# Second layer's probability transfers issued by SyncE, and the last heads' outputs moved into the output projection

## Chip, core and metric

The kernel runs on one core of a Trainium2 chip. The metric is the time of one execution on the device, in microseconds (us); the kernel before takes 2298.8 us (median of three runs, 2298.3 to 2300.2). A difference of about 0.2% (4.6 us) is what a measurement of this kernel can tell from no change.

## What is computed

A two-layer decoder trunk on 272 tokens (16 meta tokens and 256 inputs), width 2048, 16 heads of 128. Layer 0 uses forgetting attention. Layer 1, where the change lies, uses stick-breaking attention with keys and values from `w_kv`, followed by an output projection and a squared-ReLU MLP:

```python
def stick_breaking_attention(q, k, v):
    scale = HEAD_DIM ** -0.5
    outs = []
    for qs, qe in query_blocks(q.shape[1]):
        z = jnp.einsum('bqhd,bkhd->bhqk', q[:, qs:qe], k[:, :qe]).astype(jnp.float32) * scale
        ...
        log_beta = jax.nn.log_sigmoid(z)
        log_one_minus = jnp.where(mask, jax.nn.log_sigmoid(-z), 0.0)
        suffix = lax.cumsum(log_one_minus, axis=3, reverse=True) - log_one_minus
        a = jnp.where(mask, jnp.exp(log_beta + suffix), 0.0).astype(v.dtype)
        outs.append(jnp.einsum('bhqk,bkhd->bqhd', a, v[:, :qe]))
    return jnp.concatenate(outs, axis=1)
...
o = stick_breaking_attention(q, shared_k, shared_v)
h = h + o.reshape(b, length, D_MODEL) @ sb_w_o[i]
h = h + squared_relu_mlp(rms_norm(h, norm_mlp[layer]), w_up[layer], w_down[layer])
```

## The kernel before

**Matrix products.** Activations lie feature-major in SBUF, 16 chunks of 128 features by 272 (or 256) tokens. Every operand is split into a high and a low part, and a product is the sum of three: high by high, high by low, low by high. `gemm_group` (L215) makes 512 output features in four accumulators: it walks the 2048 input features in four quarters (kb 0 to 3) of 48 products each, 192 in all. The text calls a quarter by its number. `weights` (L186) loads each quarter as two halves of 512 KB by SyncE (L199, tiles `raw`, four buffers, so two quarters ahead), and splits each half: ScalarE makes the high part (L210, `whi`) and VectorE the low part (L211, `wlo`), again with four buffers. A load waits until VectorE has split the half that was in its buffer; a split waits for its load and until TensorE has used the part that was in its buffer. In quarters 0 and 3 TensorE takes the accumulators one after the other; in 1 and 2 it takes the first half of the weights for all four and then the second.

**Second layer's attention.** The loop at L696 takes four heads at a time (g = 0 to 3: heads 0-3, 4-7, 8-11, 12-15). A group is: product with the key weights (`w_kv[2g]`), scores `pz` (L717, L718), softplus, scan and exponential on ScalarE and VectorE (L723 to L728) for two pairs of heads, and the product with the value weights (`w_kv[2g+1]`, L743). TensorE needs the probabilities with keys on the partitions. They are turned without TensorE: VectorE transposes blocks of 32x32 (L451, tile `raw_p`), four transfers write them to a scratch in HBM (`turn_probabilities`, L454, `p_dram`), and two transfers read them back in the other order (`probabilities_back`, L461), one of them into the same tile `raw_p`. All six for each pair are issued by ScalarE, whose queue is in order: an issue that has to wait keeps back what stands behind it. The values go the same way for the first three groups (`squares`; L401 writes `v_dram`, L406 reads it back), also issued by ScalarE. For the last four heads there is no such return; TensorE transposes V itself (`token_major`, L379).

**Outputs.** `outputs1` (L749) splits the returned probabilities (L370 on ScalarE, L371 on VectorE), reads the values back, multiplies (`po`, L420 and L769, and a corner product through `pvc`, L756 and L767) and writes the result into `ao` (L443, L444). For g = 0 to 2 it is called inside the next group's key product, ahead of quarter 3. For g = 3 it is called after the loop, ahead of the output projection (L774), whose first group (`out_proj`, L608) needs these heads only in quarter 3.

**Order of the work.** The program is built with a scheduler that orders each engine's instructions by its own estimates. `behind` (L171) adds an ordering edge without a semaphore, so that an instruction is placed behind a given product; `issued` holds the products of the current group. The transfers back are placed behind products 140 and 184 of the value product (L744), and the splits of the returned probabilities behind products 36 and 72 of the next group, or, for the last heads, behind the last product so far (L752). Each transfer signals on one of a small number of landing semaphores, used in turn; an instruction that would signal on one again waits until the earlier transfer on it has landed, whichever engine issued it.

Of the kernel before, what the change touches and what calls it, by code (L numbers as in the profile page):

```python
# [18 lines left out]
M = 16  # L19
# [10 lines left out]
G_A0, G_M0, G_KV, G_A1, G_M1, G_FIN = range(6)  # L30
# [3 lines left out]
def yoco_kernel(ctx: ExitStack, tc: tile.TileContext, hT_in, gains, b_f, w_f, w_qkv0, w_o0, w_up, w_dn,  # L34
                w_kv, w_q1, w_o1, g_row, out):
    nc = tc.nc
# [126 lines left out]
    queued, pinned, issued = [], [False], []  # L163
# [279 lines left out]
        nc.scalar.activation(hi, src, AF.Copy)  # L443
        nc.vector.tensor_tensor(out=lo, in0=src, in1=hi.bitcast(F32), op=ALU.subtract)  # L444

    def turn_probabilities(s, raw, pr):

        y = raw[:, :768].rearrange("p (c h b i) -> p c h b i", c=4, h=2, b=3)
        for i in range(2):
            for b, o in enumerate((0, 144, 144 + P)):  # L450
                nc.vector.transpose(y[:, :, i, b, :], s[:, 2 * pr + i, o:o + P].rearrange("p (c k) -> p c k", c=4))  # L451
        y = y.rearrange("p c h b i -> p c (h b i)")
        for a in range(4):
            nc.scalar.dma_start(p_dram[pr].rearrange("c j a x -> a j c x")[a], y[32 * a:32 * a + 32])  # L454

    def probabilities_back(pps, places):
        for pr, at in enumerate(places):
            raw, p0, p1 = pps[pr]
            back = p_dram[pr].rearrange("c j a (h x) -> (c j) (a h) x", h=2)
            for dst, src in ((raw[:, :512], back[:, :, :64]), (p1.rearrange("p i q -> p (i q)"), back[:, :, 64:])):  # L460
                behind(nc.scalar.dma_start(dst.rearrange("p (m x) -> p m x", m=8), src), issued[at])  # L461

    def in_order(p0, p1):

# [4 lines left out]
    ao = Split("o0", 0)  # L469
    for g in range(4):  # L470
# [71 lines left out]
        pps = []  # L542
        for pr in range(2):
            raw = att.tile([P, 2, 2, 256], F32, tag="pp", bufs=3, name=f"raw_p0_{g}_{pr}").rearrange("p x i q -> p (x i q)")
            p0 = att.tile([P, 2, 2, 256], F32R, tag="pp", bufs=3, name=f"p0_{g}_{pr}")
            p1 = tmp.tile([P, T], F32, tag="relu", name=f"p1_{g}_{pr}")[:, :2 * P].rearrange("p (i q) -> p i q", i=2)

            turn_probabilities(s, raw, pr)
            pps.append((raw, p0, p1))


# [10 lines left out]
        gemm_group(w_qkv0[3 * g + 2], xa, 0, lambda m, acc: evac_kv(m, acc, vT))  # L562


        probabilities_back(pps, (140, 176 if g else 191))

# [12 lines left out]
        for pr in range(2):  # L581
            raw, p0, p1 = pps[pr]
# [22 lines left out]
            outputs()  # L605


    def out_proj(w, ao, t0, gi, label):  # L608
        norm = Norm(label, t0)
        xm = Split(label, t0)  # L610
        for g in range(4):
            def evac(m, acc, g=g):
                c = 4 * g + m
                residual_add(c, acc, t0)
                split_chunk(xm, gi, c)
                norm.add(c)
            gemm_group(w[g], ao, t0, evac)
        return xm, norm

    def mlp(layer, xm, norm, t0, last_evac, last_group=None):  # L620
# [75 lines left out]
    for g in range(4):  # L696
        kT = att.tile([P, 4, T], F32, tag="kT", bufs=1, name=f"kT1_{g}")
        gemm_group(w_kv[2 * g], xc, 0, lambda m, acc: evac_kv(m, acc, kT), {3: outputs1} if g else {})
        q = qT1[g]

        k0 = att.tile([P, 4, T], F32R, tag="vT", bufs=1, name=f"k0_{g}")
        k1 = ao.spare[:, 4 * g:4 * g + 4]
        for j in range(0, 4, 2):
            nc.scalar.activation(k0[:, j:j + 2], kT[:, j:j + 2], AF.Copy)
            nc.vector.tensor_tensor(out=k1[:, j:j + 2], in0=kT[:, j:j + 2], in1=k0[:, j:j + 2].bitcast(F32),
                                    op=ALU.subtract)
        q2 = att.tile([P, 2, 4, P], F32R, tag="pp", bufs=3, name=f"q12_{g}")
        split(q2, q[:, :, P:S])
        z = att.tile([P, 4, 416], F32, tag="s", bufs=1, name=f"z_{g}")

        pps = []
        for pr in range(2):
            zp = z[:, 2 * pr:2 * pr + 2]
            for i in range(2):
                j = 2 * pr + i
                ps = patt.tile([P, 512], F32, tag="patt", name=f"pz_{g}_{j}")
                product = by_parts(ps[:, 144:416], [q2[:, k, j, :] for k in range(2)], [k0[:, j], k1[:, j]], True, True)  # L717
                placed_behind(nc.tensor.matmul(ps[:, 0:144], q[:, j, 0:P], kT[:, j, :144], start=True, stop=True), product)  # L718
                nc.vector.tensor_tensor(out=z[:, j], in0=ps[:, :416], in1=maskB, op=ALU.add)
            e, raw = (att.tile([P, 2, 2, 256], F32, tag="pp", bufs=3, name=f"{x}_{g}_{pr}")  # L720
                      .rearrange("p x i q -> p (x i q)") for x in ("e", "raw_p1"))
            e, sums = e[:, :832], raw[:, :832]
            softplus(e.rearrange("p (i k) -> p i k", i=2), zp)  # L723
            nc.vector.tensor_tensor_scan(out=sums, data0=goes_on.rearrange("p i k -> p (i k)"), data1=backward(e), initial=0.0,  # L724
                                         op0=ALU.mult, op1=ALU.add)
            zf = zp.rearrange("p i k -> p (i k)")
            nc.vector.tensor_tensor(out=zf, in0=zf, in1=backward(sums), op=ALU.subtract)  # L727
            nc.scalar.activation(zp, zp, AF.Exp)  # L728

            p0 = att.tile([P, 4, T], F32R, tag=("kT", "qT")[pr], bufs=(1, 4)[pr], name=f"p01_{g}_{pr}")  # L730
            p0 = p0.rearrange("p h t -> p (h t)")[:, :1024].rearrange("p (x i q) -> p x i q", x=2, i=2)
            p1 = tmp.tile([P, T], F32, tag="relu", name=f"p11_{g}_{pr}")[:, :2 * P].rearrange("p (i q) -> p i q", i=2)
            turn_probabilities(z, raw, pr)
            pps.append((raw, p0, p1))

        pm = patt.tile([P, 512], F32, tag="patt", name=f"pm1_{g}")
        placed_behind(nc.tensor.transpose(pm[:, 0:P], corners(z[:, :, P:144], z[:, :, 400:416], f"sm1_{g}"), ident), product)
        pm_sb = att.tile([P, 192], F32, tag="pm_sb", bufs=1, name=f"pm_sb1_{g}")
        nc.vector.tensor_tensor(out=pm_sb[:, :P].rearrange("p (b q) -> p b q", q=M), in1=maskD, op=ALU.mult,
                                in0=pm[:, P - M:P].unsqueeze(1).to_broadcast([P, 8, M]))  # L740

        vT = att.tile([P, 4, T], F32, tag="vT", bufs=1, name=f"vT1_{g}")
        gemm_group(w_kv[2 * g + 1], xc, 0, lambda m, acc: evac_kv(m, acc, vT))  # L743
        probabilities_back(pps, (140, 184))  # L744
        turned = squares(vT, "pp", f"1_{g}") if g < 3 else None
        if g < 3:
            scratch(turned, issued[-2:])

        def outputs1(g=g, vT=vT, pps=pps, pm_sb=pm_sb, turned=turned):  # L749
            for pr in range(2):  # L750
                raw, p0, p1 = pps[pr]
                behind(split(p0.rearrange("p x i q -> p x (i q)"), raw[:, :512]), issued[(36, 72)[pr] if g < 3 else -1])  # L752
            if turned is not None:
                vs = values_back(turned, issued[64:80:8], issued[112:128:8], f"1_{g}")
            pv = patt.tile([P, 512], F32, tag="patt", name=f"pvc_{g}")
            nc.tensor.transpose(pv[:, :P], corners(vT[:, :, P:144], vT[:, :, 256:T], f"vc1_{g}"), ident)  # L756
            vc_sb = att.tile([P, P], F32, tag="vm_sb", bufs=1, name=f"vc_sb_{g}")
            nc.scalar.copy(vc_sb, pv[:, :P])
            own = att.tile([P, 8, M], F32, tag="own", bufs=1, name=f"own1_{g}")
            for pr in range(2):  # L760
                v0, v1 = vs[pr] if turned is not None else token_major(vT, pr, 0, f"1_{g}_{pr}")
                po = patt.tile([P, 2, 256], F32, tag="patt", name=f"po1_{g}_{pr}")
                p0, p1 = in_order(*pps[pr][1:])
                for i in range(2):
                    product = weighted(po, v0, p0, i)
                    if pr == i == 0:
                        placed_behind(nc.tensor.matmul(pv[:, P:2 * P], vc_sb, pm_sb[:, :P], start=True, stop=True), product)  # L767
                        nc.scalar.copy(own, pv[:, P:2 * P].rearrange("p (c q) -> p c q", c=8))
                    nc.tensor.matmul(po[:, i, P:], v1[:, i, :], p1[:, i], start=False, stop=i == 1)  # L769
                ends = po.rearrange("p i (c q) -> p (i c) q", c=2)[:, :, P - M:]  # L770
                nc.vector.tensor_tensor(out=ends, in0=ends, in1=own[:, 4 * pr:4 * pr + 4], op=ALU.add)
                put_split(ao, 4 * g + 2 * pr, 2, M, S, po)

        if g == 3:  # L774
            outputs1()

    xm, norm_m = out_proj(w_o1, ao, M, G_M1, "m1")


    g_tok = att.tile([P, 4, T], F32, tag="kT", bufs=1, name="g_tok").rearrange("p h t -> p (h t)")[:, :512]  # L780
# [136 lines left out]
```

## Time and profile before

| | us |
|---|---|
| runs | 2298.3, 2298.8, 2300.2 |
| profiled execution | 2298.19 |
| its span (first to last instruction) | 2296.5 |
| TensorE busy in the span | 2269.9 |
| VectorE busy | 1344.9 |
| ScalarE busy | 1058.7 |
| mean granted TensorE clock | 0.995 of full |

PE is TensorE, DVE VectorE, ACT ScalarE, POOL GpSimd, SP SyncE; L210 is line 210 of the kernel. A "q" behind an engine's name (ACTq, SPq) is its sequencer, which issues transfers. In the view of waits a row reads: engine, tile and line that waited, what released it, then total us, number of times and the longest. In the view of windows a row reads: stretch, its length, busy us and instructions of PE, weight loads, DVE, ACT and POOL, then granted clock (1.00 is full), DMA share and GB/s. In a timeline a row reads: start, duration, engine, line, operation, written<-read tiles, count, and in brackets the engine's idle time before it with what ended it. The view of one tile gives, for each instruction on it, durations in ns (minimum/median/maximum).

### The profile page before, as it was taken

Reading aid. Unit: us, or ns where it says so; the run is one execution under the profiler, and the core shown is the slowest. Engines: PE = TensorE matmul, PEld = TensorE weight load, DVE = VectorE, ACT = ScalarE, POOL = GpSimd, SP = SyncE. Lnnn points to the kernel's source line nnn. Section 1 sums busy time; section 2 is a strip of 40 time slices with the busy share of each in tenths; the row PEclk is TensorE's granted clock in tenths of the full one; section 3 lists DMA queues with packets and bytes.
Section 4 is the critical chain, followed back from the end, with each engine's and each line's share of the span. In section 5 each row is a group of like instructions: output and inputs, shape, how many; then the busy total and the mean of one; then the engine's idle time right before and its main releaser. Section 6 shows DMA issues by size and latency. Waiting matters only on the chain.

```text
span 2296.5 us, 44901 instructions
## 1 busy us (share of the span) xinstructions
PE 2269.9 (99%) x18830; PEld 2260.0 (98%) x18830; DVE 1344.9 (59%) x1943; ACT 1058.7 (46%) x1451; POOL 36.7 (2%) x78
## 2 busy tenths in 40 slices
PE   9999999999999999999999999999999999999998
PEld 9999999999999999999999999999999999999998
DVE  7766666554554455455566677666555555555555
ACT  6444455443343344344454344455543543544554
POOL 0000000000000000000000000000000000000001
PEclk9999999999999999999999999999999999999999
DMA  7766765555555555555556566666666566566564
GB/s 238 226 197 192 221 184 170 183 174 182 173 183 180 171 185 175 182 175 179 181 177 199 174 187 182 176 197 201 188 190 202 186 200 199 187 200 191 186 202 139
DMA packets 167418, 431.46 MB, mean 188 GB/s; under 512 B 48800, under 2 KB 65072, under 8 KB 167216
## 3 DMA queue, kind: packets, MB, share of 16 engines
q1 hardware_dynamic: 113760, 406.29, 55.4%
q10 hardware_dynamic: 53456, 22.31, 4.0%
q8 instruction: 147, 2.41, 0.4%
q14 instruction: 55, 0.45, 0.1%
HBM read 416.99 MB, written 11.55 MB: 187 GB/s over the span
## 4 chain that ended last, share of the span: by engine, by line
PE 94%; DVE 2%; DMA 2%; issue 1%; ACTq 1%; ACT 0%; POOL 0%; POOLq 0%; SPq 0%; DVEq 0%
PE acc L177 91%; DMA raw_p<-p_dram 1%; DVE wlo L211 1%; DMA raw<-w_qkv 1%; PE po L420 0%; DVE raw_p L724 0%; DMA p_dram<-raw_p 0%; ACT whi L210 0%; ACTq L454 0%; DVE raw_p L451 0%; ACTq L401 0%; PE pz L420 0%; PE ps L420 0%; DVE z L727 0%; DVE e L693 0%
## 5 line engine op out<-in xcount | busy, mean ns | idle before, releaser
L211 DVE TENSOR_TENSOR wlo<-raw,whi 128x1024 fp32r<-128x1024 f32 (+1 forms) x773 | 927.4, 1216 | 730.4 <-ACT whi L210 722.4
L210 ACT ACTIVATE whi<-raw 128x1024 fp32r<-128x1024 f32 (+1 forms) x773 | 795.9, 1050 | 997.8 <-PE acc L177 904.2
L177 PE MATMUL acc<-x_m,whi 128*128 128x272 f32 (+1 forms) x4096 | 643.0, 281 | 0.0
L177 PE MATMUL acc<-x_u,whi 128*128 128x272 f32 (+1 forms) x3968 | 625.9, 281 | 0.0
L177 PEld LDWEIGHTS acc<-x_m,whi 128*128 128x128 f32 x4096 | 565.7, 188 | 0.1
L177 PEld LDWEIGHTS acc<-x_u,whi 128*128 128x128 f32 x3968 | 550.1, 188 | 0.0
L177 PE MATMUL acc<-x_m,wlo 128*128 128x272 f32 (+1 forms) x2048 | 440.7, 281 | 0.0
L177 PE MATMUL acc<-x_u,wlo 128*128 128x272 f32 (+1 forms) x1984 | 431.5, 281 | 0.0
L177 PE MATMUL acc<-x_a,whi 128*128 128x272 f32 (+1 forms) x2048 | 355.2, 286 | 0.7 <-ACT whi L210 0.5
L177 PEld LDWEIGHTS acc<-x_m,wlo 128*128 128x128 f32 x2048 | 323.2, 188 | 0.0
L177 PEld LDWEIGHTS acc<-x_u,wlo 128*128 128x128 f32 x1984 | 315.1, 188 | 0.0
L177 PEld LDWEIGHTS acc<-x_a,whi 128*128 128x128 f32 x2048 | 300.7, 188 | 2.6 <-ACT whi L210 1.7
L177 PE MATMUL acc<-x_a,wlo 128*128 128x272 f32 (+1 forms) x1024 | 253.4, 285 | 0.0
L177 PE MATMUL acc<-x_kv,whi 128*128 128x272 f32 x1024 | 199.5, 294 | 14.3 <-ACT whi L210 14.3
L177 PEld LDWEIGHTS acc<-x_kv,whi 128*128 128x128 f32 x1024 | 166.0, 195 | 15.1 <-ACT whi L210 15.1
L177 PEld LDWEIGHTS acc<-x_a,wlo 128*128 128x128 f32 x1024 | 175.5, 188 | 0.7 <-DVE ssq_a L143 0.4
L177 PE MATMUL acc<-x_o,whi 128*128 128x272 f32 (+1 forms) x1024 | 162.4, 282 | 0.0
L177 PE MATMUL acc<-x_kv,wlo 128*128 128x272 f32 x512 | 150.7, 294 | 1.6 <-DVE wlo L211 1.6
L177 PEld LDWEIGHTS acc<-x_o,whi 128*128 128x128 f32 x1024 | 142.0, 188 | 0.0
L292 DVE TENSOR_TENSOR hT<-acc,hT 128x272 f32<-128x272 f32 (+1 forms) x156 | 67.4, 432 | 75.4 <-PE acc L177 75.2
L177 PE MATMUL acc<-x_o,wlo 128*128 128x272 f32 (+1 forms) x512 | 110.8, 282 | 0.0
L177 PEld LDWEIGHTS acc<-x_kv,wlo 128*128 128x128 f32 x512 | 99.7, 195 | 2.5 <-DVE wlo L211 2.5
(220 smaller groups left out, 1042.4 us busy)
## 6 DMA issues: line engine op xcount, KB each, us to landing
raw<-w_up SPq DMA_DIRECT2D x256, 512.0 KB, 3.9
raw<-w_dn SPq DMA_DIRECT2D x256, 512.0 KB, 3.9
raw<-w_qkv SPq DMA_DIRECT2D x92, 512.0 KB, 4.1
raw<-w_o SPq DMA_DIRECT2D x64, 512.0 KB, 4.1
raw<-w_kv SPq DMA_DIRECT2D x64, 512.0 KB, 4.3
raw<-w_q SPq DMA_DIRECT2D x32, 512.0 KB, 4.7
p_dram<-raw_p ACTq DMA_DIRECT2D x64, 96.0 KB, 4.1
raw_p<-p_dram ACTq DMA_DIRECT2D x16, 256.0 KB, 6.7
```

What stands on the lines that cost most here:

```text
L177: ins = nc.tensor.matmul(*args, **kw).ins
L210: on_act = nc.scalar.activation(hp, src, AF.Copy)
L211: on_dve = nc.vector.tensor_tensor(out=lp, in0=src, in1=hp.bitcast(F32), op=ALU.subtract)
L292: nc.vector.tensor_tensor(out=hT[:, c, t0:], in0=acc, in1=hT[:, c, t0:], op=ALU.add)
```

## The change

Two edits. `turn_probabilities` and `probabilities_back` take the issuing queue as an argument: layer 0 passes ScalarE's as before, layer 1 passes SyncE's. And `outputs1` of the last heads is no longer called ahead of the output projection but inside its first group, ahead of quarter 1, with its two splits placed behind products 20 and 40 of that group. The values' transfers (L401, L406) stay on ScalarE.

```diff
-    def turn_probabilities(s, raw, pr):
+    def turn_probabilities(s, raw, pr, queue):
...
-            nc.scalar.dma_start(p_dram[pr].rearrange("c j a x -> a j c x")[a], y[32 * a:32 * a + 32])
+            queue.dma_start(p_dram[pr].rearrange("c j a x -> a j c x")[a], y[32 * a:32 * a + 32])
...
-    def probabilities_back(pps, places):
+    def probabilities_back(pps, places, queue):
...
-                behind(nc.scalar.dma_start(dst.rearrange("p (m x) -> p m x", m=8), src), issued[at])
+                behind(queue.dma_start(dst.rearrange("p (m x) -> p m x", m=8), src), issued[at])
...
-    def out_proj(w, ao, t0, gi, label):
+    def out_proj(w, ao, t0, gi, label, before={}):
...
-            gemm_group(w[g], ao, t0, evac)
+            gemm_group(w[g], ao, t0, evac, before if g == 0 else {})
...
-            turn_probabilities(z, raw, pr)
+            turn_probabilities(z, raw, pr, nc.sync)
...
-        probabilities_back(pps, (140, 184))
+        probabilities_back(pps, (140, 184), nc.sync)
...
-                behind(split(p0.rearrange("p x i q -> p x (i q)"), raw[:, :512]), issued[(36, 72)[pr] if g < 3 else -1])
+                behind(split(p0.rearrange("p x i q -> p x (i q)"), raw[:, :512]), issued[((36, 72) if g < 3 else (20, 40))[pr]])
...
-        if g == 3:
-            outputs1()
-
-    xm, norm_m = out_proj(w_o1, ao, M, G_M1, "m1")
+    xm, norm_m = out_proj(w_o1, ao, M, G_M1, "m1", {1: outputs1})
```

More of the change, by code (lines that the diff above doesn't have):

```diff
@@ L546, in yoco_kernel @@
             p1 = tmp.tile([P, T], F32, tag="relu", name=f"p1_{g}_{pr}")[:, :2 * P].rearrange("p (i q) -> p i q", i=2)
-            turn_probabilities(s, raw, pr)
+            turn_probabilities(s, raw, pr, nc.scalar)
             pps.append((raw, p0, p1))
@@ L562, in yoco_kernel @@
         gemm_group(w_qkv0[3 * g + 2], xa, 0, lambda m, acc: evac_kv(m, acc, vT))
-        probabilities_back(pps, (140, 176 if g else 191))
+        probabilities_back(pps, (140, 176 if g else 191), nc.scalar)
         pv = patt.tile([P, 512], F32, tag="patt", name=f"pvm_{g}")
```

## Prediction

> **What bounds the kernel now.** I read the page's first lines, then TensorE's waits in the second layer (span 1236 to 1512 us), then the stretches around them, then ScalarE's timeline inside the longest.
>
> ```profile
> span 2296.5 us, 44901 instructions
> PE 94%; DVE 2%; DMA 2%; issue 1%; ACTq 1%; ACT 0%; POOL 0%; POOLq 0%; SPq 0%; DVEq 0%
> ...
> PE acc L177 <- ACT whi L210: 14.3, 3, 5.8
> PE pvc L756 <- POOL pk_vc L438: 2.7, 1, 2.7
> PE acc L177 <- DVE wlo L211: 1.6, 3, 0.7
> ...
> 1293.05:1354.50 61.45, 55.20 (x431) 54.64 (x430) 40.89 (x67) 28.40 (x37) 1.71 (x4) 0.94 0.64 181
> 1354.50:1415.20 60.70, 55.71 (x430) 55.15 (x430) 40.81 (x67) 28.40 (x37) 1.77 (x4) 0.94 0.65 182
> 1415.20:1476.00 60.80, 56.06 (x431) 55.60 (x430) 40.89 (x67) 28.50 (x37) 1.87 (x4) 0.94 0.63 182
> 1323.70:1328.50 4.80, 4.36 (x18) 4.04 (x19) 4.80 (x5) 3.93 (x6) 0.00 (x0) 0.50 0.81 243
> 1383.90:1389.90 6.00, 5.56 (x23) 5.24 (x24) 5.72 (x6) 3.90 (x6) 0.00 (x0) 0.50 0.88 262
> 1445.30:1451.40 6.10, 6.10 (x27) 6.10 (x28) 4.51 (x5) 3.66 (x7) 0.00 (x0) 0.50 0.93 285
> 1498.40:1501.00 2.60, 0.00 (x0) 0.00 (x0) 1.24 (x3) 1.17 (x2) 0.41 (x2) 1.00 0.59 121
> ```
>
> TensorE is the bound; only its waits and its clock can be won. In the second layer it waits 14.3 + 1.6 us in three places, one for each of heads 0-3, 4-7 and 8-11, and 2.7 us once at the last heads. In the rows of windows the last three columns are granted clock, DMA share and GB/s. Behind each of the three waits the clock is 0.50, for 4.36, 5.56 and 6.10 us of busy time: half of that, 8.0 us, is lost too. The 2.7 us wait left the clock at 1.00. Check: each group's stretch less its own wait and half-clock loss (61.45 - 6.25 - 2.18, 60.70 - 4.99 - 2.78, 60.80 - 4.74 - 3.05; the single waits are in the next fence) is 53.0, 52.9 and 53.0 us, the same work three times. So **24.0 us** lie in three groups and **2.7 us** at the last one.
>
> ```profile
> 1302.56 2.21 ACTq L454 DMA_DIRECT2D p_dram<-raw_p  x4
> ...
> 1308.92 0.54 ACTq L461 DMA_DIRECT2D raw_p<-p_dram  x1
> 1309.50 0.68 ACTq L461 DMA_DIRECT2D p<-p_dram  x1
> 1310.33 6.32 ACTq L454 DMA_DIRECT2D p_dram<-raw_p  x4
> 1316.75 2.39 ACTq L401 DMA_DIRECT2D v_dram<-turned  x5
> 1319.26 0.53 ACTq L461 DMA_DIRECT2D raw_p<-p_dram  x1
> ...
> 1322.53 1.06 ACT L210 ACTIVATE whi<-raw 128x1024 fp32r<-128x1024 f32 x1 [14.86 <-DMA raw_p<-p_dram]
> ...
> 1323.64 0.82 PE L177 MATMUL acc<-x_kv,whi 128*128 128x272 f32 x2 [5.81 <-ACT whi L210]
> ...
> 1383.81 0.60 PE L177 MATMUL acc<-x_kv,whi 128*128 128x272 f32 x1 [4.55 <-ACT whi L210]
> ...
> 1444.00 0.52 PE L177 MATMUL acc<-x_kv,whi 128*128 128x272 f32 x2 [3.99 <-ACT whi L210]
> 1445.26 0.60 PE L177 MATMUL acc<-x_kv,wlo 128*128 128x272 f32 x1 [0.75 <-DVE wlo L211]
> ```
>
> The cause stands in ScalarE's queue (the short second waits are 0.75 in the third group, and the rest of 1.6, so 0.44 each, in the other two). An issue that has to wait for an earlier transfer (L461 for L454's landing, the second L454 for its transposes) keeps every later ScalarE instruction waiting. The weight split L210 of the next group's second quarter (kb 1) stands behind all of them and comes 14.86 us late.
>
> **The change part by part.** Removed from ScalarE in each of four groups: 8 issues L454 and 4 issues L461. The same 12 go to SyncE, between weight loads. The instruction order built from the changed program shows the rest. On ScalarE the split of kb 1's first half now stands ahead of all value issues L401, so it can run when TensorE has left the buffer that it reuses, one quarter (48 products) earlier. TensorE wants it at 1317.57 + 0.27 = 1317.84.
>
> ```profile
> 1301.26 1.27 DVE L451 STREAM_TRANSPOSE raw_p<-z 128x128 f32<-128x128 f32 x6
> ...
> 1309.03 1.27 DVE L451 STREAM_TRANSPOSE raw_p<-z 128x128 f32<-128x128 f32 x6
> ...
> 1317.57 0.27 PE L756 MATMUL pvc<-ident,pk_vc 128*128 128x128 f32 x1
> ...
> 1308.80 0.33 SPq L199 DMA_DIRECT2D raw<-w_kv  x1
> ...
> L454 ACTq DMA_DIRECT2D p_dram<-raw_p x32: 315/478/4042, 1302.6 to 1499.9; - x32
> ...
> L211 DVE TENSOR_TENSOR wlo<-raw,whi x48: 1180/1219/1227, 1294.2 to 1469.9; 128x1024 fp32r<-128x1024 f32 x48
> DMA to landing us min/median/max: 3.4/4.3/6.7
> ...
> L401 ACTq DMA_DIRECT2D v_dram<-turned x24: 309/454/916, 1316.7 to 1442.3; - x24
> DMA to landing us min/median/max: 1.7/2.2/3.1
> ...
> 428.32 756.84 PE acc L177 x6144
> 1599.71 533.27 PE acc L177 x4704
> ```
>
> (The two landing rows are those of the weight tiles and of the value tiles; a product takes 756.84 / 6144 = 0.123 us with 272 columns, 533.27 / 4704 = 0.113 us with 256.) Three new couplings have to be priced, on the first group's clock. A time from the median issue comes first; after the slash, one in which SyncE is held 4.04 us behind L461, as ScalarE was once (maximum of the L454 row).
>
> 1. **Weights behind transfers on SyncE.** L461 of pair 0 waits for L454's landing; I keep the 1308.9 of before, since transposes and transfer are the same. It takes 1.2 us to issue. Behind it stand the loads of kb 2, until now issued by 1308.80: now about 1310.5 / 1314.3, landed 4.3 us later at 1314.8 / 1318.6. Kb 2 is wanted at 1317.84 + 48 x 0.123 = 1323.8, so this alone costs nothing.
> 2. **Values behind those weights on ScalarE.** Landing semaphores are shared in turn, so in the new order the last L401 of pair 0 waits for the second kb 2 load, and the split of kb 1's second half stands behind it. It would end at 1314.8 + 0.45 + 1.06 = 1316.3 / 1320.1, and VectorE's half 1.22 us later at 1317.5 / 1321.4. TensorE wants them at 1317.84 + 24 x 0.123 = 1320.8 and 1321.0. Cost 0 / 0.4 us. Kb 2's split then follows a 0.6 us split of probabilities and four more L401, which wait for the first ones' landing (2.2 us): about 1320 / 1323 for ScalarE's part, 1324.1 at the latest for VectorE's, against 1323.8: 0 / 0.3 us.
> 3. **Last pair at the products `po`.** L461 of pair 1 waits for its L454 (transposes end 1310.3; issued by 1312.8 / 1316.5; 4.1 us more to L461, as from 1302.56 + 2.21 to 1308.92), so it issues near 1316.9 / 1320.6, against 1319.26 before. Kb 3's first load comes behind its 1.2 us (and the 4.04 us) and lands near 1322.8 / 1330.2; the value return L406 of pair 1 stands behind that load's split and takes 2.2 us and 0.8 us of its own split, so these values are there by about 1325.8 / 1333.2. `po` of pair 1 runs near 1317.84 + 96 x 0.123 + 1 = 1330.7. Cost 0 / 1.8 us beyond the 0.7 of step 2.
>
> So each group keeps 0 to 2.5 us. I take 0.5, near the lower end, because only one of 32 issues took 4 us. No single wait then reaches 2.67 us, after which the clock was still 1.00 (1498.40 row), so the 8.0 us of half clock go as well. Sum for three groups: 24.0 - 3 x 0.5 = **22.5 us**. VectorE and ScalarE can follow: 40.89 and 28.40 us of work in 53.
>
> [...]
>
> **The last heads.** Here the second L454 follows a split that waits 8.09 us for L461's landing, and VectorE stands behind the same split with the last quarter of V, so POOL's corner copy and `pvc` are late.
>
> ```profile
> 1485.50 2.03 ACTq L454 DMA_DIRECT2D p_dram<-raw_p  x4
> ...
> 1498.55 0.63 ACT L370 ACTIVATE p<-raw_p 128x512 fp32r<-128x512 f32 x1 [8.09 <-DMA raw_p<-p_dram]
> ...
> 1501.96 0.54 ACTq L461 DMA_DIRECT2D raw_p<-p_dram  x1
> ...
> 1505.86 0.64 ACT L370 ACTIVATE p<-raw_p 128x512 fp32r<-128x512 f32 x1
> ...
> 1500.59 0.42 POOL L438 COPY pk_vc<-vT 128x64 f32<-128x64 f32 x2 [5.50 <-DVE vT L480]
> ...
> 1501.06 0.33 PE L756 MATMUL pvc<-ident,pk_vc 128*128 128x128 f32 x1 [2.67 <-POOL pk_vc L438]
> ```
>
> Called after kb 0, with the splits placed behind products 20 and 40, V's last quarter goes ahead of the split and `pvc` stands after 48 products instead of 32: the 2.67 us go. In their place the first `po` stands after product 85 and needs a value split that is queued on ScalarE behind pair 1's probabilities. The group's first product ran at 1498.38 - 32 x 0.113 = 1494.8 and product 85 ends near 1494.8 + 9.6 + 0.5 (my estimate for `pvc` and four transposes) = 1504.9. By step 3, moved on by 1485.50 - 1302.56 = 182.9, L461 of pair 1 issues near 1499.8 / 1503.5, against 1501.96 before; it has landed at most 3.9 us later (1501.96 to 1505.86), and two splits take 1.0: the values are there at 1504.7 / 1508.4. New wait 0 to 3.5 us; I take 1.2, nearer the lower end for the reason given. Net gain 2.7 - 1.2 = **1.5 us**. Quarter 3 wants the last heads only after product 144, some 2 us after they are done.
>
> **Sum.** 22.5 + 1.5 = 24.0 us. The profiled execution took 2298.2 us (span 2296.5 and 1.7 around it), 0.6 under the median of the three runs. 2298.2 - 24.0 = **2274.2 us**.
>
> **The rivals.**
> *Waits come back elsewhere.* Steps 2 and 3 at their upper ends, 2.5 us in each of three groups, and as much lost at the last heads as won: 24.0 - 7.5 = 16.5, giving 2281.7; with the clock drop in one group (3 us) 2285. For it: steps 2 and 3 leave about 1 to 3 us of room at the medians. Against: TensorE no longer meets ScalarE's 14.86 us.
> *It only saves the issuing.* The transfers get no faster, and if ScalarE still stands as long for L401's landings, only 8 x 0.478 + 2 x 1.22 = 6.3 us of issue leave its queue; the waits of 4 to 5.8 us just go, unless the loads slip by as much. If they do slip, waits and half clock stay and only the last heads' 1.5 us are won: 2296.7.
> [...]
> *Slower: SyncE's order starves kb 1.* The mechanism of step 2, further on: if the second kb 2 load lands after about 1319.3, TensorE waits from 1320.8. It loses what was won (8.0 us a group) when the landing is near 1324.3 (5 us of wait and 3 of half clock). At 1327, 8 us and 3 in each group: 3 x 3 us slower, 2307. Against: that is 8 us behind the upper bound above, and more than any landing row shows.
>
> **How the numbers follow.** Forecast case (2271.5 to 2278): 0.64. Waits elsewhere (2278 to 2287): 0.22. Only the issuing (2294 to 2298): 0.06. Slower: 0.08. The range must leave out no more than 0.2: 2271.5, where nothing is left of all 26.7 us, less 0.5 for the run, is 2271; above it reaches into the second case, to 2285. A measurement here tells 0.2%, 4.6 us, from no change: faster 0.87, same 0.05, slower 0.08.
>
> **What would show it.** ScalarE's 14.86 us before L210 gone; windows of the three groups near 53 to 55 us with clock 1.00; TensorE's waits for L210 under 1 us each; a wait of 1 to 2 us before `po` (L420) in the output projection's first group; L454 and L461 as SyncE issues. Wrong if the clock shows 0.50 again there, or if SyncE's loads of kb 2 land after 1319 on the first group's clock.

## The result and the profile after

| | before | changed |
|---|---|---|
| median of 4 runs each, same chip, us | 2299.5 (2298.3 to 2301.7) | 2274.1 (2273.6 to 2274.6) |
| ratio, 95% interval | | 0.9888 (0.9871 to 0.9906) |
| profiled execution, us | 2298.2 | 2274.0 |
| mean granted clock | 0.995 | 1.000 |

The changed kernel is 1.1% faster, by 24.2 us between the two profiled executions; the prediction said 24.0 and 2274.2 us. The number holds. Its parts hold less well, as the runs below show.

First the changed kernel's span, then all waits of TensorE in the second layer (engine, tile, line, releaser; total us, times, longest), then the windows of the three groups (length; busy us of PE, weight loads, DVE, ACT, POOL; clock, DMA share, GB/s):

```profile
span 2272.3 us, 44903 instructions
```

```profile
PE po L420 <- ACT v L370: 0.9, 1, 0.9
PE po L420 <- DVE v L371: 0.2, 1, 0.2
```

```profile
1293.42:1346.90 53.48, 53.16 (x430) 52.76 (x429) 40.69 (x67) 28.93 (x38) 1.76 (x4) 1.00 0.70 207
1346.90:1400.40 53.50, 53.26 (x431) 52.85 (x430) 40.73 (x67) 29.02 (x38) 1.76 (x4) 1.00 0.67 207
1400.40:1453.10 52.70, 52.70 (x430) 52.70 (x430) 40.64 (x67) 28.90 (x38) 1.76 (x4) 1.00 0.70 210
```

The reader is to see three things. Not one wait for L210 or L211 is left. The groups take 53.5, 53.5 and 52.7 us where they took 61.5, 60.7 and 60.8, close to the 53 us that the prediction had worked out as the work alone. And the clock is 1.00 in all three. (The view of waits lists only larger ones; the groups' remainders at `po` are 0.32, 0.24 and 0 us, the first two read as length less busy time.) The first group starts at 1293.42 instead of 1292.5, so 0.9 us were lost ahead of it, in work that the change doesn't touch. That is spread: in `e1` below, which differs from neither ahead of this place, the group starts at 1291.8.

ScalarE's timeline (start, us, engine, line, operation, written<-read, count, idle time before it and what ended it) shows the new order in the first group:

```profile
1311.79 1.06 ACT L210 ACTIVATE whi<-raw 128x1024 fp32r<-128x1024 f32 x1 [2.48 <-PE acc L177]
1312.54 4.18 ACTq L401 DMA_DIRECT2D v_dram<-turned  x4
1316.84 1.06 ACT L210 ACTIVATE whi<-raw 128x1024 fp32r<-128x1024 f32 x1 [4.00 <-DMA p_dram<-raw_p]
...
1319.52 2.01 ACT L210 ACTIVATE whi<-raw 128x1024 fp32r<-128x1024 f32 x2 [1.10 <-DMA v_dram<-turned]
1322.01 0.34 ACTq L406 DMA_DIRECT2D turned<-v_dram  x1
```

The first half of the kb 1 split runs at 1311.79 as soon as TensorE frees its buffer; before, it ran at 1322.53, after 14.86 us. The second half stands behind four value issues that take 4.18 us in all: the wait that the prediction called coupling 2, real, and ended in time. On SyncE, in order:

```profile
1307.31 0.61 SPq L461 DMA_DIRECT2D raw_p<-p_dram  x1
...
1308.71 1.93 SPq L199 DMA_DIRECT2D raw<-w_kv  x2
1311.07 2.13 SPq L454 DMA_DIRECT2D p_dram<-raw_p  x4
1318.13 0.53 SPq L461 DMA_DIRECT2D raw_p<-p_dram  x1
```

The two L199 are the loads of kb 2. The profile gives one landing for them, 6.2 us after the issue, and the second issue began at 1310.2. So that load was there at about 1316.4, between the prediction's 1314.8 and 1318.6; the fourth value issue, which waits for it in the built program, left at 1316.4.

### The profile page after: what moved, and what is told of

Same layout as the page of the kernel before. It is cut to its first block, busy times and chain, and to the rows that moved or that the text cites. A ratio compares the mean times of both kernels' runs of the same rounds, so it can differ in the third digit from the quotient of the medians.

```text
span 2272.3 us, 44903 instructions
## 1 busy us (share of the span) xinstructions
PE 2263.1 (100%) x18830; PEld 2254.2 (99%) x18830; DVE 1344.1 (59%) x1943; ACT 1060.1 (47%) x1451; POOL 37.5 (2%) x78
## 4 chain that ended last, share of the span: by engine, by line
PE 95%; DMA 2%; DVE 1%; issue 0%; ACT 0%; SPq 0%; ACTq 0%; POOL 0%; POOLq 0%; DVEq 0%
PE acc L177 93%; DMA p_dram<-raw_p 1%; DMA turned<-v_dram 1%; DMA raw<-w_qkv 1%; PE po L420 0%; DMA raw_p<-p_dram 0%; ACT whi L210 0%; DVE wlo L211 0%; PE ps L420 0%; PE pz L420 0%; DMA raw<-w_kv 0%; DMA v_dram<-turned 0%; DVE raw_p L451 0%; PE pz L718 0%; PE ps L516 0%
## 5 line engine op out<-in xcount | busy, mean ns | idle before, releaser
L211 DVE TENSOR_TENSOR wlo<-raw,whi 128x1024 fp32r<-128x1024 f32 (+1 forms) x773 | 927.6, 1216 | 704.9 <-ACT whi L210 697.7
L210 ACT ACTIVATE whi<-raw 128x1024 fp32r<-128x1024 f32 (+1 forms) x773 | 796.4, 1050 | 966.1 <-PE acc L177 912.8
L177 PE MATMUL acc<-x_kv,whi 128*128 128x272 f32 x1024 | 193.9, 288 | 0.0
L177 PEld LDWEIGHTS acc<-x_kv,whi 128*128 128x128 f32 x1024 | 160.7, 188 | 0.0
```

Source lines behind the costliest of these rows:

```text
L177: ins = nc.tensor.matmul(*args, **kw).ins
L210: on_act = nc.scalar.activation(hp, src, AF.Copy)
L211: on_dve = nc.vector.tensor_tensor(out=lp, in0=src, in1=hp.bitcast(F32), op=ALU.subtract)
```

## The experiments

The theories, as they stood when the runs were chosen:

- **A**: ScalarE's issues that wait for landings (L461 above all) made the kb 1 split late; taking them away gives three groups' waits and half clock, about 23 us, and the last heads' move some 2 us.
- **B**: the move of the last heads paid.
- **C**: only the issuing time that leaves ScalarE counts, the rival "It only saves the issuing" that the prediction weighed.
- **A2**, formed after the first four runs: what counts is which issues the kb 1 split stands behind on ScalarE, whichever engine issues the probabilities.
- **D**, its rival: the probabilities must leave ScalarE.

### The two edits apart

`e1`: the queues alone. From the kernel before, with both helpers taking the queue as in the change:

```diff
-            turn_probabilities(z, raw, pr)
+            turn_probabilities(z, raw, pr, nc.sync)
...
-        probabilities_back(pps, (140, 184))
+        probabilities_back(pps, (140, 184), nc.sync)
```

> Only the issuing queue changes: the second layer's probability transfers (L454, L461) go to SyncE, the last heads stay ahead of the output projection. Theory A (waits inside ScalarE's issues made the kb 1 split late): the three groups' waits at TensorE (15.9 us) fall under 1 us in all, the clock stays at 1.00, so 2299.5 - 23.4 = about 2276 us, with the 2.7 us wait at pvc mostly still there. Theory B (the last heads' move is what paid): about 2297 us. Theory C (only issuing time counts): all issues of the second layer have left ScalarE here, so 2276 too; this run does not tell A from C.

Measured: 2273.6 us, ratio 0.9886 (0.9871 to 0.9901). This is the whole gain, with nothing left for the move. TensorE's waits in its second layer, then two instructions around the last heads (ScalarE, GpSimd):

```profile
PE po L420 <- ACT v L370: 2.4, 3, 1.1
```

```profile
1471.43 0.63 ACT L370 ACTIVATE p<-raw_p 128x512 fp32r<-128x512 f32 x1 [1.75 <-DMA raw_p<-p_dram]
```

```profile
1473.82 2.27 POOL L438 COPY pk_vc<-vT 128x64 f32<-128x64 f32 x2 [0.42 <-DVE vT L480]
```

There is no wait at `pvc` any more, although the last heads are where they were. The split that stood 8.09 us for the returned probabilities stands 1.75, V's last quarter is not held behind it, and the corner copy comes in time: the same delay of the transfers had fed that wait too. The 2.4 us that are left stand at `po` of the first two groups, where the expectation had under 1 us in all. B falls.

`e2`: the move alone (the edits of L749 and L774 of the diff, every transfer on ScalarE).

> Only the last heads' outputs move into the first group of the output projection; all transfers stay on ScalarE. Theory A: the three waits for L210 of 4 to 5.8 us and the stretches of clock 0.50 stay, the 2.7 us at pvc go and a wait of 0 to 3.5 us before po comes: 2296 to 2300 us, most likely near 2297.7 (1.8 us won, as in the changed kernel). Theory B: about 2276 us.

Measured: 2295.4 us, ratio 0.9988 (0.9978 to 0.9997).

```profile
PE acc L177 <- ACT whi L210: 13.8, 3, 5.0
PE acc L177 <- DVE wlo L211: 1.9, 3, 0.7
PE po L769 <- ACT v L383: 1.0, 1, 1.0
```

The three groups are as before; 2.7 us at `pvc` have become 1.0 at `po`. The move is worth something only as long as the transfers are late: 3.1 us between the medians alone, none on top of the queues.

### Half of the queues

Both with the move, and one of the two helpers on SyncE.

```diff
-            turn_probabilities(z, raw, pr, nc.sync)
+            turn_probabilities(z, raw, pr, nc.scalar)
```

> The move of the last heads, and of the queues only the transfers back (L461) on SyncE; the writes L454 stay on ScalarE. In the instruction order ScalarE still issues both L454 and all value issues L401 ahead of the kb 1 split, but no longer stands for L454's landing. Theory A: the split comes near 1319 us on the first group's clock instead of 1322.5, TensorE waits 1.5 to 3 us in each group and the clock stays at 1.00: 2278 to 2283 us. Theory C (the gain goes with the issuing time that leaves ScalarE, of which L461 is 2 x 1.22 of 6.3 us a group): 1.8 + 0.39 x 22.3 = 10.5 us won, 2289 us.

Measured: 2295.4 us, ratio 0.9983 (0.9973 to 0.9992): both theories missed. TensorE's waits, ScalarE's and SyncE's timelines:

```profile
PE acc L177 <- ACT whi L210: 11.8, 3, 4.5
PE acc L177 <- DVE wlo L211: 1.9, 3, 0.7
PE po L420 <- ACT v L370: 1.8, 1, 1.8
```

```profile
1309.71 1.92 ACTq L454 DMA_DIRECT2D p_dram<-raw_p  x4
1312.13 8.41 ACTq L401 DMA_DIRECT2D v_dram<-turned  x8
1320.64 1.06 ACT L210 ACTIVATE whi<-raw 128x1024 fp32r<-128x1024 f32 x1 [13.73 <-DMA v_dram<-turned]
```

```profile
1309.97 1.26 SPq L199 DMA_DIRECT2D raw<-w_kv  x2
```

L461 has left ScalarE, and the split is late all the same, because the eight value issues now stand for 8.41 us themselves. In the built program the first two wait for the landing of pair 0's transfers back and the next two for the loads of kb 2, with which they share landing semaphores and which SyncE issues only behind its L461. In the trace those loads are issued from 1309.97 on, and the last of the eight value issues has left at 1320.54. The wait has moved to the next issue in the queue. A as put forward falls: it isn't L461's own wait that decides.

```diff
-        probabilities_back(pps, (140, 184), nc.sync)
+        probabilities_back(pps, (140, 184), nc.scalar)
```

> The move of the last heads, and of the queues only the writes (L454) on SyncE; the transfers back (L461), which wait for landings, stay on ScalarE. In the instruction order the kb 1 split now stands ahead of all value issues and of pair 1's L461; pair 0's L461 stands ahead of the second half of the kb 0 split. Theory A (a wait costs only what is due behind it): nothing due for long stands behind L461 any more, 0 to 2 us a group are lost, 2274 to 2280 us. Theory C: L454 is 8 x 0.478 of 6.3 us of issuing a group, so 1.8 + 0.61 x 22.3 = 15.4 us won, 2284 us.

Measured: 2284.7 us, ratio 0.9939 (0.9922 to 0.9955). The number is that of C, but not for C's reason:

```profile
PE po L420 <- ACT v L370: 3.1, 1, 3.1
PE acc L177 <- DVE wlo L211: 2.2, 3, 0.7
PE acc L177 <- ACT whi L210: 1.1, 2, 0.6
```

```profile
1487.70:1491.70 4.00, 4.00 (x19) 4.00 (x20) 2.71 (x4) 2.19 (x5) 0.00 (x0) 0.50 0.75 247
```

The three groups lose 3.3 us together, as A expected (0 to 2 each). What is missing was lost at the last heads: 3.1 us at `po`, and half clock behind it. With the waits of 6.4 us instead of 1.4 and some 3 us for the clock (2 of them in the window shown), its profiled execution of 2281.7 us against 2274.0 is accounted for; the median lies 3 us higher than that execution, which no profile explains.

### The order on ScalarE alone

`e5`: the kernel before, all issues on ScalarE, and ordering edges (no semaphores) that put the value issues and pair 1's L461 behind the kb 1 split:

```diff
+            if u in (55, 57, 59) and kb == 1:
+                for x in late[-10:]:
+                    behind(x, on_act.ins)
...
```

(`late` collects the eight L401 and pair 1's two L461 of the group; 55, 57 and 59 number the key products of heads 4-7, 8-11 and 12-15.)

> The kernel before with every transfer still issued by ScalarE and the last heads where they were; only ordering edges are added, so that in the three groups both halves of the kb 1 split stand ahead of the value issues (L401) and of pair 1's transfer back (L461), but still behind pair 0's L461 and both L454. Theory A2 (formed after the run with only L461 on SyncE: what counts is what the kb 1 split stands behind, whichever queue the probabilities use): the split runs when the last L454 has left, near 1316.7 us on the first group's clock, so TensorE waits about 1 to 2 us there and perhaps 1 to 2 at kb 2 and po, with the clock at 1.00; the 2.7 us at the last heads stay: 2280 to 2288 us. Theory D (the transfers must leave ScalarE): 2294 to 2299 us.

Measured: 2281.2 us, ratio 0.9929 (0.9912 to 0.9947). TensorE's waits and ScalarE's timeline (lines are shifted: L460 is L454, L426 is L420, L765 is L756):

```profile
PE acc L177 <- DVE wlo L211: 2.6, 5, 0.7
PE pvc L765 <- POOL pk_vc L444: 2.5, 1, 2.5
PE po L426 <- ACT v L373: 1.1, 1, 1.1
PE acc L177 <- ACT whi L210: 1.0, 1, 1.0
```

```profile
1310.17 5.37 ACTq L460 DMA_DIRECT2D p_dram<-raw_p  x4
1315.65 1.06 ACT L210 ACTIVATE whi<-raw 128x1024 fp32r<-128x1024 f32 x1 [8.25 <-DMA p_dram<-raw_p]
```

No issue has left ScalarE, and 16.8 of the 25 us are won. So C and D fall as the whole cause: the place of one split in one queue is enough to take most of the loss away. The waits that remain sum to 7.1 us, 5.7 more than in the changed kernel, and the clock stays at 1.00 behind them.

`e5r` is the reverse: the changed kernel with the kb 1 split put behind the last value issue.

```diff
+                if u in (55, 57, 59) and kb == 1:
+                    behind(on_act, last_out[0])
...
```

> The changed kernel with all its transfers of probabilities on SyncE, and one ordering edge more: in the three groups the kb 1 split stands behind the last value issue L401 on ScalarE, as it did in the kernel before. Theory A2: the value issues wait for the landings of the kb 2 loads and of the first values, the split comes near 1320 us, TensorE waits about 4 us and loses half clock again in each group, only the last heads' part stays won: 2291 to 2297 us. Theory D (what counts is that ScalarE no longer issues the probabilities): near 2274 us.

Measured: 2283.3 us, ratio 0.9933 (0.9918 to 0.9947), between the two. Waits and timeline (L405 is L401, L213 is L211):

```profile
PE acc L177 <- ACT whi L210: 5.3, 3, 2.5
PE acc L177 <- DVE wlo L213: 2.2, 3, 0.7
```

```profile
1311.22 7.49 ACTq L405 DMA_DIRECT2D v_dram<-turned  x8
1318.82 1.06 ACT L210 ACTIVATE whi<-raw 128x1024 fp32r<-128x1024 f32 x1 [10.82 <-DMA v_dram<-turned]
```

A2's direction holds, its size was too large: the value issues stand 7.49 us and the split comes 1.8 us earlier than with L461 alone on SyncE. The mere place of the split costs 9 us between this median and the changed kernel's. But 14.7 us of the gain over the kernel before stay although the split is where it was: with the probabilities gone from ScalarE it has less ahead of it, 10.82 us of idle time in place of 14.86. So either step alone, the order (`e5`, 16.8 us) or the queues (`e5r`), wins well over half, and the two do not add up. What they have in common is that the split comes sooner, at 1315.7 and 1318.8 us in place of 1322.5; in `e5r` the wait at the last heads is gone as well.

### Half clock by itself

`f1`: the kernel before, with products on data at hand in the three waits; their results are used by nothing.

```diff
+            if kb == 1 and u in (55, 57, 59):
+                keep = patt.tile([P, 512], F32, tag="patt", name=f"keep_{u}")
+                for _ in range(26):
+                    ins = nc.tensor.matmul(keep[:, :n], sp.hi[:, 0, :P], sp.hi[:, 0], start=True, stop=True).ins
...
```

> The kernel before with 26 products of 272 columns (26 x 0.123 = 3.2 us) added ahead of kb 1 in the three groups, on data that is there already, their results unused; TensorE then idles for at most 2.6 us instead of 5.8. The weight split comes when it came before. If the half clock follows from the idle time: clock 1.00 behind the wait, 8.0 us won and the waits' 15.9 us kept, about 2299 - 8 = 2291 us. If the clock falls for another reason (DMA traffic, the work behind): no gain, or up to 3 x 3.2 us lost, 2299 to 2308 us.

Measured: 2295.0 us, ratio 0.9985 (0.9976 to 0.9995): 3 us won, not 8. TensorE's timeline in the first group, then the clock behind it:

```profile
1317.32 3.42 PE L234 MATMUL keep<-x_kv 128*128 128x272 f32 x26
...
1322.18 0.51 PE L177 MATMUL acc<-x_kv,whi 128*128 128x272 f32 x2 [1.34 <-ACT whi L210]
1323.45 0.59 PE L177 MATMUL acc<-x_kv,wlo 128*128 128x272 f32 x1 [0.75 <-DVE wlo L211]
```

```profile
1323.50:1326.50 3.00, 3.00 (x13) 3.00 (x14) 3.00 (x3) 2.67 (x5) 0.00 (x0) 0.50 0.85 283
...
1381.00:1384.00 3.00, 2.22 (x15) 2.00 (x16) 2.98 (x3) 3.00 (x4) 0.00 (x0) 1.00 0.59 138
```

Only the second group, left with 0.15 and 0.75 us of wait, kept its clock. In the first, 1.34 and 0.75 us were enough for half clock; the third, with 2.19 and 0.74, lost it too. That TensorE's idle time matters for the clock is shown by the second group: 1.00 here from 1384 to 1390 us, 0.50 before from 1383.9 to 1389.9, with nothing changed there but the added work. That waits under 2.67 us are always safe is refuted.

### How much room SyncE has

`e6`: the changed kernel with the loads of kb 2 behind pair 1's transfers back, the mechanism of the rival on the slower side.

```diff
+                if u in (55, 57, 59) and kb == 2:
+                    behind(ins, last_back[0])
...
```

> The changed kernel with the loads of kb 2 of the three groups placed behind pair 1's transfers back on SyncE (the mechanism of the rival on the slower side: SyncE's in-order queue holds the weights). In the order that comes out the second half of the kb 1 split also stands behind all value issues, of which the last one waits for pair 1's L461 to land, near 1323 us. If the mechanism is real: that half is ready near 1324 to 1325 us where TensorE wants it at 1320.8, so 3.5 to 5 us of wait and 0 to 3 us of half clock a group: 2284 to 2298 us. If SyncE's order has room to spare: near 2274 us.

Measured: 2271.5 us, ratio 0.9884 (0.9869 to 0.9899): no loss at all. The view of TensorE's waits in its second layer is empty. SyncE's timeline (L456 is L454, L465 is L461):

```profile
1309.96 1.77 SPq L456 DMA_DIRECT2D p_dram<-raw_p  x4
1313.47 0.52 SPq L465 DMA_DIRECT2D raw_p<-p_dram  x1
1314.04 0.67 SPq L465 DMA_DIRECT2D p<-p_dram  x1
1314.76 14.66 SPq L199 DMA_DIRECT2D raw<-w_kv  x8
```

Pair 1's transfer back goes out 3.5 us after the first of its writes; in the changed kernel it took 7.1 us (1311.07 to 1318.13). In the built programs it waits for the landing of its pair's writes (in `e6` also of pair 0's return). What was moved from ahead of these small writes are the loads of kb 2, and the DMA engines are less full there:

```profile
1308.70:1312.70 4.00, 4.00 (x35) 4.00 (x34) 4.00 (x16) 1.52 (x2) 0.42 (x2) 1.00 0.99 178
```

```profile
1309.90:1313.40 3.50, 3.50 (x31) 3.50 (x30) 3.50 (x13) 1.06 (x1) 1.03 (x1) 1.00 0.71 159
```

(The changed kernel and `e6`, the stretches of pair 1's writes: DMA share 0.99 and 0.71.) So the chain that the loads were put behind got 3.6 us shorter. The loads still went out 6 us later (1314.76 against 1308.71), and they were in time: the first is used at 1320.7, and TensorE wants kb 2 only after kb 1's 48 products. The first branch of the expectation had kept the old length of that chain, and is off by 12 us or more.

The last four ran on one chip: the changed kernel again, `e6` again, `e6` without the move of the last heads, and the changed kernel with the first layer's probabilities on SyncE too.

```diff
-            turn_probabilities(s, raw, pr, nc.scalar)
+            turn_probabilities(s, raw, pr, nc.sync)
...
-        probabilities_back(pps, (140, 176 if g else 191), nc.scalar)
+        probabilities_back(pps, (140, 176 if g else 191), nc.sync)
```

> The changed kernel once more, as the measure for the other three on the same chip: 2273 to 2275 us.

> The changed kernel with the loads of kb 2 behind pair 1's transfers back, once more. In its first run the second layer's waits at TensorE were 0.12 us in place of the changed kernel's 1.45, since pair 1's writes no longer share the DMA engines with those loads and L461 of pair 1 went out 4.7 us earlier. If the waits are all there is to it: 1.3 us under the changed kernel; if the 2.6 us between the two medians so far are more than spread: 2.6 us under it; if it is spread: no difference.

> The same with the last heads' outputs back ahead of the output projection, their splits behind the last product so far. The prediction gave the move 1.5 us of its own: then 1.5 us above the run with the move. If SyncE's queue alone had already taken away the wait at the last heads, as the run with the queues alone shows: no difference, 2270 to 2273 us.

> The changed kernel with the first layer's probability transfers on SyncE too. In the first layer ScalarE's issues wait as well, but TensorE waits nowhere behind them (0.34 us at pom in the changed kernel). If an issue's wait costs only where something due stands behind it: no difference, 2272 to 2276 us. If SyncE's in-order queue starves the weights where it waits: 1 to 8 us slower in each of four groups, 2278 us or more.

| | us, median (lowest to highest of 4) | ratio, 95% interval |
|---|---|---|
| changed kernel again | 2274.0 (2272.2 to 2275.6) | 0.9899 (0.9882 to 0.9915) |
| `e6` again | 2272.2 (2271.9 to 2274.2) | 0.9890 (0.9876 to 0.9905) |
| `e6` without the move | 2272.5 (2271.5 to 2273.2) | 0.9889 (0.9875 to 0.9904) |
| first layer's too | 2273.0 (2271.3 to 2275.7) | 0.9893 (0.9878 to 0.9908) |

All four are one time within the 0.2% that can be told. `e6` was the fastest both times it ran, by 2.6 and 1.8 us, but the intervals overlap, and its profiled executions had 0 and 1.0 us of waits in the second layer against 1.1 and 0.9: it is faster than the kernel before, but that it is faster than the changed kernel isn't shown. The move is not needed. In the first layer taking ScalarE's waiting issues away won nothing that can be told: the view of before has no wait of TensorE there, from 20 to 1236 us.

## Why the prediction was right, and where it wasn't

**What bounds, and the 24.0 us.** Right. Waits and half clock of the three groups, 24.0 us less the 0.56 that stay, were nearly the whole gain, and the groups came down to the 53 us computed from before.

**The cause.** Right in the main sentence: the kb 1 split stood behind issues that keep it waiting. `e5` shows it with no issue moved away. But which issues decide was told only in part. L461 alone can go without any gain (`e3`), as the value issues behind it then wait in its place. The new order of ScalarE's queue, which the prediction read off the built program, wins 16.8 us by itself (`e5`); the issues' leaving wins 14.7 us without it (`e5r`). One reading is off: it isn't the transposes that keep the second L454. They end at 1309.03 + 1.27 = 1310.30, and it starts at 1310.33; its four issues themselves take 6.32 us, one of them 4.04, where four of the median 0.478 take 1.9. They take 5.37 us in `e5`, still on ScalarE, and 2.13 on SyncE in the changed kernel. What makes them long on ScalarE no run here shows.

**Coupling 1 and 2**, cost 0 / 0 to 0.7. Right: the kb 2 loads came within the bounds, the second half of the kb 1 split ended at 1316.84 + 1.06 = 1317.9 where 1316.3 to 1320.1 was written (0.9 of it is the group's later start), and no wait for L210 or L211 remained.

**Coupling 3**, 0.5 us taken a group. The place is right (`po`), the size is 0.56 us in all against 1.5, and one duration in it was far too short. The prediction put the risk on pair 1's values; in the first group, the chain of the changed kernel that ended last runs over pair 0's:

```profile
1312.72 4.12 DMA p_dram<-raw_p
...
1318.13 3.79 DMA raw_p<-p_dram
1322.01 7.19 DMA turned<-v_dram
```

The value return took 7.19 us. Of the six of the second layer the profile gives two landings, 7.2 and 7.0 us; the other four were used 4.9 to 7.5 us after their issue, at the end of a wait for them (pair 1's here issued at 1324.75, used at 1331.38); the prediction had put 2.2, from a row in which writes and returns stand together. In the kernel before, the returns alone (L406) land in 2.7 to 2.9 us where the profile gives a landing. There SyncE issues no load between 1308.80 and 1324.88 us; here the first return comes among pair 1's return and four weight loads, issued from 1318.13 to 1323.3. That this company is the reason is argued, not shown. The sum also left out the split of kb 3's first half itself (1.06 us), behind which pair 1's return stands.

**The half clock.** The 8.0 us went, as said. The reason given, that no single wait reaches 2.67 us, was too weak a test: `f1` lost its clock after 1.34 and 0.75 us, `e3` after 1.80. The changed kernel's longest wait is 0.9 us, and no profiled execution here lost its clock after so little.

**The last heads, net 1.5 us.** The sum held (2.7 less 0.9 is 1.8), the step failed. "Called after kb 0 ... the 2.67 us go" gave the gain to the move, while the prediction's own sentence ahead of it had named the cause, a split that waits 8.09 us for L461's landing. `e1` shows that the queues end that wait and `pvc` with it; the move then only puts a wait at `po` of 0.2 to 0.9 us there. The two edits were priced as if their gains added up: measured alone they are worth 24.9 and 3.1 us, together 25.4.

**The sum.** Against the predicted 24.0 us: 0.9 less lost in the groups, 0.3 less at the last heads, 0.9 more lost ahead of the second layer's first group, so 24.3, and 24.2 measured. The agreement within 0.2 us is partly luck: these terms cancel, and the 0.9 is spread.

**The rivals.** "Waits come back elsewhere": couplings 2 and 3 are real, and ended within 1 us; it did come true in `e3` and `e4`, where half of the transfers moved. "It only saves the issuing": `e5` wins 16.8 us with no issue saved. This kernel's time was in the work that stood behind a waiting issue: the kb 1 split ran after 14.86 us of idle time, and in the changed kernel after 2.48. "SyncE's order starves kb 1": `e6` brought its condition about, since kb 2's loads issued behind pair 1's transfers were first used at 1320.7, and nothing was lost. The break-even point of the rival rested on a landing semaphore shared between those loads and the value issues, and with the loads moved the built program pairs the semaphores in another way. So that chain itself was made late in no run.

What stays open: why the medians of `e6` lie 2 us under the changed kernel's both times, if that is more than spread, what made the second L454 long on ScalarE, and the 3 us by which `e4`'s median exceeds its profiled execution.

## What to carry to other kernels

Read what is late from the queue that it stands in, and ask for each waiting issue ahead of it what would wait next if that one were gone: here taking away one of two waits won nothing, while reordering alone won two thirds. Before pricing two edits by their sum, look whether both gains hang on the same late transfer. And a bulk load that isn't due yet can be put behind a small transfer that is: here the small one then went out 3.6 us sooner, and the load, 6 us later, was still in time.

## What the runs showed of the hardware

**Half clock after much shorter waits than thought, and not after some longer ones.** `e3`, behind a single wait of 1.80 us at `po` (1501.43 to 1503.23), `e5`, behind one of 2.50 us at `pvc` (to 1483.08), and `e5r`, around the waits of 1.47 and 0.75 us ahead of kb 1 in its second group (1375.45 to 1378.18):

```profile
1504.30:1507.60 3.30, 3.10 (x15) 2.81 (x15) 1.38 (x2) 2.47 (x4) 0.00 (x0) 0.50 0.98 360
```

```profile
1483.20:1486.50 3.30, 3.30 (x30) 3.30 (x31) 2.72 (x3) 2.51 (x5) 0.00 (x0) 1.00 0.43 83
```

```profile
1376.00:1380.00 4.00, 2.34 (x16) 2.12 (x17) 3.10 (x3) 4.00 (x5) 0.00 (x0) 1.00 0.99 242
```

The short wait cost 1.6 us more in half clock (3.10 us of busy time at 0.50), the longer one nothing, and before's 2.67 us nothing either. `e5r`'s 1.47 and 0.75 us cost nothing, where `f1`'s 1.34 and 0.75 did. So the length of a wait alone does not decide. In `e3` the piece at half clock begins about 1 us after the wait has ended: TensorE runs again from 1503.23, and the clock is still 1.00 from 1503.50 to 1504.30. What decides besides the length no run here shows.

**Small transfers behind bulk loads.** Four writes of 96 KB and the issue that waits for them took 3.5 us where 7.1 were needed behind two loads of 512 KB (`e6` and the changed kernel), on the same issuing engine.
